# The way down of a SwiGLU FFN in seven products over all tiles of h, with GpSimd forming the sums

## The chip, the cores and the metric

The kernel runs on one core of a Trainium2 chip. The metric is the device time of one execution in microseconds. TensorE (PE in the profile) multiplies matrices into PSUM; VectorE (DVE), ScalarE (ACT) and GpSimd (POOL) do elementwise work; SyncE (SP) holds the queue from which every transfer of this kernel is issued, in order.

## The reference

One layer of a hybrid encoder: two token mixers, a gated merge, a layer norm, and the FFN to which the change belongs.

```python
x = layer_norm(DEEPNORM_ALPHA * x + mix, ln1_g[l], ln1_b[l])
gu = x @ w_ffn_in[l]
g, u = jnp.split(gu, 2, axis=-1)
ffn = (jax.nn.silu(g) * u) @ w_ffn_out[l]
x = layer_norm(DEEPNORM_ALPHA * x + ffn, ln2_g[l], ln2_b[l])
```

x is 1024 x 1024, h = silu(g) * u is 1024 x 2816, all in float32. A product of float32 precision is made of three products of rounded parts: each operand a is split into a high part (a cast on ScalarE to the format fp32r) and a low part (a subtraction on VectorE), and hi*hi, hi*lo and lo*hi are added up in PSUM.

## The kernel before, in words

Sequence, model width and FFN width are cut into tiles of 128. A slot is an SBUF buffer of 128 x 1024 float32; slots come in tags (`bw`, `pt`, `yt`, `kp`, `op`, `xt`, `gt` and the group `QKV` of four tags with two each), and a tile gets one when an earlier tile of its tag is done with. A bank is a PSUM buffer of 128 x 512 (tags `mm`, `sc`, `tr`, `pv`; eight in all). A scheduler at build time fixes the order of each engine's queue: it takes the program's order as priority and moves up what its own estimate shows to be ready. On the chip each queue then runs in that order and waits by semaphores.

**The way up** (`up_steps`, `pair_steps`, `run_pairs`) makes h transposed, tile f = 0..21: rows are 128 features of h, columns the 1024 positions. Tile f of the gate and tile f of the up half form a pair of 2 x 2 blocks, multiplied by the seven products of Strassen's scheme in Winograd's form, in the order 1, 2, 6, 5, 7, 3, 4; each is 12 TensorE products of 128 x 128 by 128 x 512. Names in the profile: `sxf`, `syf` and `szf` are the banks (`sxf` takes products 1, 6, 7, 4, `szf` 5 and 3, `syf` 2), `wLf` and `wRf` the loaded weights, `wlf`, `waf`, `wbf` and `wcf` their split operands, `gt` and `h` the results. Between products ScalarE or VectorE read the bank, which goes on adding up. `right` and `left` load and prepare the weights of the next two pairs. A finished h tile is stored to `h_dr`.

**The way down** multiplies h by `w_ffn_out` (2816 x 1024). The 22 tiles of h are taken in six groups (2, then five times 4). For a group, its h tiles (`wr_h`) and the matching rows of `w_ffn_out` (`wr_fo`) are loaded and split whole (`wh_`, `wl_`); then for each of the 8 row tiles and both column halves one bank (`fps`) takes all products of the group, and VectorE adds it to `acc_t`, which held x1, the FFN's input (slots `op`, loaded from `x1_dr`). After the last group each row tile is normalised by `layer_norm` and stored: statistics, a power on GpSimd, a scaling on ScalarE, the addition of `ln2_b` on GpSimd; the last tile takes a quick form on VectorE.

Of the kernel before, what the change touches and what calls it, by code (L numbers as in the profile page):

```python
# [11 lines left out]
F32 = mybir.dt.float32  # L12
# [12 lines left out]
N_REL = 513  # L25
D_FF = 2816
NF = D_FF // P
ALPHA = 2.0 ** 0.25
EPS = 1e-5
BIG = 1e30  # L30
# [16 lines left out]
def hybrid_trunk_kernel(ctx: ExitStack, tc, x, xt, w_in, b_gate, rel_bias, w_proj,  # L47
# [14 lines left out]
    def slot(tag, name, dtype=F32):  # L62
        return pool.tile([P, 1024], dtype, tag=tag, name=name, bufs=SLOTS[tag])
# [32 lines left out]
    g_dr = dram("g_dr", 16)  # L96
    m_dr = dram("m_dr", 8)
    x1_dr = dram("x1_dr", 8)
    h_dr = dram("h_dr", NF)
    rel_dr = dr.tile([8, 896], F32, name="rel_dr")  # L100

    def split(dst_h, dst_l, src):
        nc.scalar.copy(dst_h, src)  # L103
        nc.vector.tensor_tensor(dst_l, src, dst_h.bitcast(F32), ALU.subtract)  # L104
# [283 lines left out]
    def load_w(srcs, name, raw, hl, lo_eng):  # L388
        r = raw(f"wr_{name}")
        hi = hl(f"wh_{name}", F32R)  # L390
        lo = hl(f"wl_{name}", F32R)
        srcs = srcs if isinstance(srcs, list) else [(slice(0, 1024), srcs)]
        for cs, src in srcs:
            dma(r[:, cs], src)
        nc.scalar.copy(hi, r)  # L395
        lo_eng.tensor_tensor(lo, r, hi.bitcast(F32), ALU.subtract)
        return hi, lo

    def of(tag):
        return lambda name, dtype=F32: slot(tag, name, dtype)  # L400
# [404 lines left out]
    def right_f(f):  # L805
        prep_right(Wf[f], f"f{f}", w_ffn_in[NF + f], ("bw", "pt")[f % 2],
                   "op" if f == 1 else None)
        if f:
            prep_last(Wf[f], f"f{f}", "op")

    def up_steps(f):
# [12 lines left out]

        def done(name, acc):
            if name == "11":
                nc.scalar.activation(c("11"), c("11"), AF.Silu)
            elif name == "12":
                nc.vector.tensor_tensor(c("12"), c("12"), c("11"), ALU.mult)
            elif name == "21":  # L830
                h = tl["h"]
                nc.scalar.activation(h[:, HI], acc, AF.Silu)
                nc.vector.tensor_tensor(h[:, HI], h[:, HI], c("22"), ALU.mult)
                dma(h_dr[f], h)

        return pair_steps(f"f{f}", Wf[f], ops_1, c, done, "pv" if f == 2 else "mm")

# [31 lines left out]
    down_tags = [("bw",) * 2 + ("kp",) * 2, QKV + ("bw", "bw", "pt", "pt"), ("xt",)]  # L869
    for gi, (f0, f1) in enumerate(groups):  # L870
        hs = []
        tags = down_tags[0 if gi == 0 else 1 + gi % 2]
        take = lambda name, dtype: cycle(tags, name, dtype)
        for f in range(f0, f1):
            hs.append(load_w(h_dr[f], f"h{f}", of("gt"), take, nc.vector) +
                      load_w(w_ffn_out[f * P:(f + 1) * P, :], f"fo{f}", of("gt"), take,
                             nc.vector))
        if f1 == NF:
            norm2 = [bcast(src, slot("yt", f"ln2{n}")) for src, n in ((ln2_g, "g"), (ln2_b, "b"))]
        for tt in range(8):  # L880
            if gi == 0:
                dma(acc_t[tt], x1_dr[tt])
            ts_ = slice(tt * P, (tt + 1) * P)
            for hf, cs in enumerate((LO, HI)):
                acc = bank("mm" if hf == 0 else "tr", f"fps{gi}_{tt}_{hf}")
                mm3(acc, [(hh[:, ts_], hl[:, ts_], oh[:, cs], ol[:, cs])
                          for hh, hl, oh, ol in hs])
                if gi == 0:
                    nc.vector.scalar_tensor_tensor(acc_t[tt][:, cs], acc_t[tt][:, cs], ALPHA,
                                                   acc, ALU.mult, ALU.add)  # L890
                else:
                    nc.vector.tensor_tensor(acc_t[tt][:, cs], acc, acc_t[tt][:, cs], ALU.add)  # L892
            if f1 == NF:
                layer_norm(acc_t[tt], *norm2, f"2_{tt}", tt == 7,
                           lambda cs: dma(out[tt * P:(tt + 1) * P, cs], acc_t[tt][:, cs]))


def granules(w):
# [31 lines left out]
```

## Time and profile before

| | |
|---|---|
| median of 3 runs (lowest, highest) | 1504.65 us (1503.48, 1505.57) |
| span of the profiled execution | 1506.8 us |
| TensorE / VectorE / ScalarE / GpSimd busy | 97% / 63% / 43% / 17% |
| mean granted TensorE clock | 0.994 |
| way up, last products before the way down | to 1259.3 us |
| way down, first to last product | 1259.3 to 1498.4 us |
| bytes moved | 202 MB, 134 GB/s over the span |

The execution that was profiled has no time of its own beside its span; the runs' times are of other executions. In a row of the profile's groups stand the line of the kernel, the engine, the operation, output and inputs by name, the count, and durations; `[idle <- X]` is how long the engine stood still before it and what ended that. A row of the stages gives the stretch, its length, then busy time and count for PE, PEld (weight loads), DVE, ACT and POOL, the granted clock, and the share and rate of the transfers.

### The profile page before, as it was taken

The numbers are of one execution on the slowest core, as the hardware profiler recorded it, in microseconds if no ns is written. First come the engines' busy times: TensorE is split into PE (matmuls) and PEld (weight loads), VectorE is DVE, ScalarE is ACT, GpSimd is POOL, SyncE is SP. The second block draws the span as 40 slices with busy tenths as digits, with TensorE's granted clock in tenths as the row PEclk, the third lists the DMA queues.
The fourth block names the chain that finished last, engine by engine and source line by source line (L and its number), as shares of the span: only waits on it lengthen the run. The fifth ranks groups of instructions, "written<-read, shape, count | busy, mean of one in ns | idle before, by whom it ended". The sixth has DMA issues, their size and how long they took to land.

```text
span 1506.8 us, 18782 instructions
## 1 busy us (share of the span) xinstructions
PE 1463.4 (97%) x6860; PEld 1204.9 (80%) x6860; DVE 945.1 (63%) x1533; ACT 645.2 (43%) x1112; POOL 255.8 (17%) x296
## 2 busy tenths in 40 slices
PE   8999999999999999999999899999999999999997
PEld 6788888787777888787887688888888888888886
DVE  8865556376677677786849975555555547354437
ACT  6444444476676567765303543333333334021201
POOL 0000000243345556840014000000000000000016
PEclk9999999999999999999999999999999999999999
DMA  6555554755554545657502132222222248032202
GB/s 210 168 169 168 167 168 159 237 162 142 154 154 126 156 135 172 209 183 277 197 6 93 57 140 85 84 84 84 84 84 81 80 151 303 29 126 98 71 5 107
DMA packets 59325, 202.09 MB, mean 134 GB/s; under 512 B 7632, under 2 KB 7632, under 8 KB 59232
## 3 DMA queue, kind: packets, MB, share of 16 engines
q1 hardware_dynamic: 59232, 200.89, 41.0%
q8 instruction: 54, 0.88, 0.2%
q14 instruction: 39, 0.32, 0.1%
HBM read 141.06 MB, written 59.80 MB: 133 GB/s over the span
## 4 chain that ended last, share of the span: by engine, by line
PE 82%; DVE 8%; ACT 3%; DMA 3%; issue 2%; POOL 1%; SPq 0%; POOLq 0%; DVEq 0%; ACTq 0%
PE sxf L165 15%; PE sxp L165 9%; PE szf L165 8%; PE gps L412 5%; PE fps L113 5%; PE fps L111 5%; PE fps L110 5%; PE szp L165 5%; PE syf L165 4%; PE syp L165 2%; PE yAps L600 2%; PE tp_b L550 2%; PE ops L113 2%; PE ops L111 2%; PE ops L110 2%
## 5 line engine op out<-in xcount | busy, mean ns | idle before, releaser
L744 POOL TENSOR_TENSOR mv<-mv,neghalf 128x1 f32<-128x1 f32 x16 | 23.7, 1479 | 763.4 <-DVE mv L743 763.4
L110 PE MATMUL fps<-wh_fo,wh_h 128*128 128x512 f32 x352 | 136.9, 389 | 0.0
L111 PE MATMUL fps<-wl_fo,wh_h 128*128 128x512 f32 x352 | 136.9, 389 | 0.0
L113 PE MATMUL fps<-wh_fo,wl_h 128*128 128x512 f32 x352 | 136.9, 389 | 0.0
L892 DVE TENSOR_TENSOR x<-fps,x 128x512 f32<-128x512 f32 x80 | 55.1, 689 | 97.0 <-PE fps L113 97.0
L529 POOL TENSOR_TENSOR w_b<-w_b,kp_b 128x511 f32<-128x511 f32 (+3 forms) x96 | 99.3, 1038 | 64.9 <-DVE kp_b L527 39.1
L527 DVE TENSOR_TENSOR_SCAN kp_b<-kp_b,ident_ps 128x384 f32<-128x384 f32 (+6 forms) x88 | 78.4, 891 | 4.6
L412 PE MATMUL gps<-xh,wl_g 128*128 128x512 f32 x192 | 80.9, 421 | 0.0
L412 PE MATMUL gps<-xh,wh_g 128*128 128x512 f32 x192 | 80.5, 419 | 0.0
L412 PE MATMUL gps<-xl,wh_g 128*128 128x512 f32 x192 | 80.5, 419 | 0.0
L111 PEld LDWEIGHTS fps<-wl_fo,wh_h 128*128 128x128 f32 x352 | 66.1, 188 | 13.8
L110 PEld LDWEIGHTS fps<-wh_fo,wh_h 128*128 128x128 f32 x352 | 66.1, 188 | 13.7
L113 PEld LDWEIGHTS fps<-wh_fo,wl_h 128*128 128x128 f32 x352 | 66.1, 188 | 13.7
L395 ACT CAST wh_h<-wr_h 128x1024 fp32r<-128x1024 f32 x22 | 23.1, 1052 | 118.7 <-PE fps L111 93.6
L519 ACT ACTIVATE kp_b<-sc_b 128x512 f32<-128x512 f32 (+3 forms) x96 | 48.3, 503 | 45.2 <-PE sc_b L456 33.8
L104 DVE TENSOR_TENSOR pt_b<-tp_b,pt_b 128x512 fp32r<-128x512 f32 (+1 forms) x96 | 51.0, 542 | 19.2 <-ACT pt_b L103 19.0
L494 POOL TENSOR_SCALAR w_a<-w_a,st_a 128x640 f32<-128x640 f32 (+2 forms) x64 | 46.4, 728 | 82.7 <-DVE st_a L493 69.9
L165 PE MATMUL szf<-x1S63h,wcf 128*128 128x512 f32 x176 | 57.8, 389 | 0.0
L103 ACT CAST pt_b<-tp_b 128x512 fp32r<-128x512 f32 (+1 forms) x96 | 47.8, 498 | 21.6 <-PE tp_b L550 21.4
L550 PE MATMUL tp_b<-ident,w_b 128*128 128x128 f32 x288 | 48.8, 277 | 4.2 <-DVE pt_b L104 1.8
L104 DVE TENSOR_TENSOR pt_a<-tp_a,pt_a 128x512 fp32r<-128x512 f32 (+1 forms) x96 | 45.6, 485 | 10.3 <-ACT pt_a L103 10.2
L178 DVE TENSOR_TENSOR gt<-sxf,gt 128x512 f32<-128x512 f32 x22 | 15.1, 688 | 58.5 <-PE sxf L165 58.5
(1535 smaller groups left out, 4192.8 us busy)
## 6 DMA issues: line engine op xcount, KB each, us to landing
wLf<-in_w_ffn_in_dram SPq DMA_DIRECT2D x22, 512.0 KB, 3.6
wRf<-in_w_ffn_in_dram SPq DMA_DIRECT2D x22, 512.0 KB, 3.6
h_dr<-h SPq DMA_DIRECT2D x22, 512.0 KB, 2.6
wr_h<-h_dr SPq DMA_DIRECT2D x22, 512.0 KB, 4.3
wr_fo<-in_w_ffn_out_dram SPq DMA_DIRECT2D x22, 512.0 KB, 4.3
v_dr<-v SPq DMA_DIRECT2D x16, 512.0 KB, 3.5
kl<-k_dr SPq DMA_DIRECT2D x32, 256.0 KB, 6.2
v<-v_dr SPq DMA_DIRECT2D x16, 512.0 KB, 3.2
```

The lines of the kernel that those rows point to most:

```text
L103: nc.scalar.copy(dst_h, src)
L104: nc.vector.tensor_tensor(dst_l, src, dst_h.bitcast(F32), ALU.subtract)
L110: mm(acc, lh, rh, start=(i == 0), stop=False)
L111: mm(acc, lh, rl, start=False, stop=False)
L113: mm(acc, ll, rh, start=False, stop=(i == n))
L165: mm(acc, lw[:, ks], rx, start=(first and kt == i == 0), stop=(kt == 3 and i == 2), skip_group_check=not first)
L412: mm(acc, lw[:, ks], rx[k][:, cs], start=(k == j == 0), stop=(k == KT - 1 and j == 2))
L519: nc.scalar.activation(kp[:, c0:e], sc[:, 0:n], AF.Sigmoid, scale=-1.0)
L527: nc.vector.tensor_tensor_scan(kp[:, s0:e], kp[:, s0:e], ident_ps()[:, 0:e - s0], kp[:, s0 - 1:s0], ALU.mult, ALU.bypass)
L529: nc.gpsimd.tensor_tensor(be[:, m0:e], be[:, m0:e], kp[:, m0 - 1:e - 1], ALU.mult)
L550: tr(tp[:, (qb - lo_q) * P:(qb - lo_q + 1) * P], wt[qb - q0][:, (kb - qb) * P:(kb - qb + 1) * P], ident)
L892: nc.vector.tensor_tensor(acc_t[tt][:, cs], acc, acc_t[tt][:, cs], ALU.add)
```

## The change

h is no longer multiplied group by group. Its 22 tiles and the 22 row blocks of `w_ffn_out` form 11 pairs, i = 0..10; the two tiles of a pair, each cut into two halves of the positions, are the 2 x 2 blocks on the left, the two row blocks, each cut into two halves of the columns, those on the right. The seven products are made one after another, each over all 11 pairs: a step is one pair in one product, 4 row tiles x 3 = 12 TensorE products. Product 1 is kept in four banks (`xbank`), in which products 6, 7 and 4 go on adding; product 2 and then product 5 take the other four (`zbank`), and 3 goes on from 5. After each product the four banks are added into `acc_t`. In product 4 the row tiles come one after another, each over all 11 pairs.

The left sums are made on GpSimd at the end of each second pair of the way up (`left_sums`), and seven halves of 128 x 512 a pair are stored to `left_dr`, in place of whole tiles to `h_dr`. The right sums are made on GpSimd from the loaded row blocks, in their own place (`right_sums`). Each step loads its left half (two to a `gt` slot) and splits both operands into slots `kp`, `QKV` and others (`split_left`, `split_right`). h of the even tiles from 4 on lies in a `bw` slot.

The core of the diff:

```diff
+NP2 = NF // 2
+ORDER = (1, 2, 6, 5, 7, 3, 4)
...
+    def left_sums(i):
+        ha, hb = h_of.pop(2 * i), h_of.pop(2 * i + 1)
+        sa, sb = slot("op", f"sa{i}"), slot("op", f"sb{i}")
+        add = nc.gpsimd.tensor_tensor
+        add(sb[:, LO], ha[:, LO], ha[:, HI], ALU.subtract)
+        add(sa[:, LO], ha[:, HI], hb[:, HI], ALU.add)
+        add(sa[:, HI], sa[:, LO], ha[:, LO], ALU.subtract)
+        add(sb[:, HI], hb[:, LO], sa[:, HI], ALU.subtract)
+        for p, t in ((1, ha[:, LO]), (2, hb[:, LO]), (4, hb[:, HI]), (5, sa[:, LO]),
+                     (6, sa[:, HI]), (7, sb[:, LO]), (3, sb[:, HI])):
+            dma(left_dr[p, i], t)
...
-                    tl["h"] = slot("yt", f"h{f}")
+                    tl["h"] = slot("bw" if f % 2 == 0 and f > 2 else "yt", f"h{f}")
...
-                dma(h_dr[f], h)
+                if f % 2:
+                    left_sums(f // 2)
...
-    groups = [(0, 2), (2, 6), (6, 10), (10, 14), (14, 18), (18, 22)]
...
+    row_tags = iter([("xt",)] * 16 + [("bw",)] * 6)
+    steps = [(p, i) for p in ORDER for i in range(NP2)]
...
+    def right_sums(s):
+        p, i = steps[s]
+        tt = nc.gpsimd.tensor_tensor
+        a, b = rows[0][i], rows[1][i]
+        if p == 2:
+            tt(a[:, LO], a[:, HI], a[:, LO], ALU.subtract)
+        elif p == 6:
+            t = t2[i] = slot("kp", f"t2_{i}")[:, LO]
+            tt(t, b[:, HI], a[:, LO], ALU.subtract)
+            tt(b[:, LO], b[:, LO], t, ALU.subtract)
+        elif p == 5:
+            tt(a[:, HI], b[:, HI], a[:, HI], ALU.subtract)
...
+    def split_left(s):
+        p, i = steps[s]
+        tags = next(wide) if p == 4 else next(first_tags, QKV)
+        ops["l", s] = split_to(tags, f"dl{p}_{i}", raw_l.pop((p, i)))
...
+    def triple(acc, s, mt, first, last):
+        l, r = ops["l", s], ops["r", s]
+        lh, ll = (l[:, o + mt * P:o + (mt + 1) * P] for o in (0, HW))
+        for n, (lw, rx) in enumerate(((lh, r[:, LO]), (lh, r[:, HI]), (ll, r[:, LO]))):
+            mm(acc, lw, rx, start=(first and n == 0), stop=(last and n == 2),
+               skip_group_check=steps[s][0] not in (1, 2, 5))
...
+    AHEAD = dict(load=9, sums=4, split=3)
+    base = {p: n * NP2 for n, p in enumerate(ORDER)}
...
+    def feed(s):
+        p, i = steps[s]
+        advance("load", s + AHEAD["load"] + (NP2 if p in (5, 7, 3) else 0), load)
+        advance("sums", s + AHEAD["sums"], right_sums)
+        for d in range(AHEAD["split"] + 1):
+            advance("l", s + d, split_left)
+            advance("r", s + d, split_right)
...
+    for s, (p, i) in enumerate(steps[:base[4]]):
+        feed(s)
+        if p == 3:
+            advance("l", base[4] + i, split_left)
+            advance("r", base[4] + i, split_right)
...
+        banks = zbank if p in (2, 5, 3) else xbank
+        for mt in range(4):
+            triple(banks[mt], s, mt, p in (1, 2, 5) and i == 0, i == NP2 - 1)
...
+    for mt in range(4):
+        for i in range(NP2):
+            triple(xbank[mt], base[4] + i, mt, False, i == NP2 - 1)
+        take(4 + mt, LO, xbank[mt], True)
+        end_row(4 + mt)
```

Three places where the order of the queues is another. The first is the way up around pair 12. SyncE's queue before, one store to each pair (the number behind `wLf`, `wRf` and `h` is f):

```order
L124 DMA wLf15_9794<-in_w_ffn_in_dram 128x1024
L137 DMA wRf15_9885<-in_w_ffn_in_dram 128x1024
L834 DMA h_dr11_160<-h11_9562 128x1024
L124 DMA wLf16_9919<-in_w_ffn_in_dram 128x1024
L137 DMA wRf16_10010<-in_w_ffn_in_dram 128x1024
L834 DMA h_dr12_161<-h12_9687 128x1024
```

SyncE's queue now (in `left_dr` the first number is the product, the second the pair of tiles; `sa` and `sb` are the sums):

```order
L140 DMA wRf14_9880<-in_w_ffn_in_dram 128x1024
L827 DMA left_dr1_5_184<-h10_9547 128x512
L827 DMA left_dr7_5_188<-sb5_9729 128x512
L827 DMA left_dr2_5_185<-h11_9671 128x512
L827 DMA left_dr4_5_190<-h11_9671 128x512
L827 DMA left_dr5_5_187<-sa5_9728 128x512
L827 DMA left_dr6_5_186<-sa5_9728 128x512
L827 DMA left_dr3_5_189<-sb5_9729 128x512
L127 DMA wLf15_9914<-in_w_ffn_in_dram 128x1024
L140 DMA wRf15_10017<-in_w_ffn_in_dram 128x1024
```

The load of `wLf15` stood ahead of the store of h11 and now stands behind the seven stores of tiles 10 and 11. ScalarE's queue in pair 12, before:

```order
L182 COPY gt12_9633<-sxf12_9620 128x512
L103 CAST wcf14_9776<-wRf14_9760 128x512
L103 CAST wlf15h_9796<-wLf15_9794 128x1024
L827 ACTIVATE gt12_9633<-gt12_9633 128x512
L191 COPY h12_9687<-sxf12_9620 128x512
L195 COPY gt12_9633<-szf12_9689 128x512
```

ScalarE's queue in pair 12 now:

```order
L185 COPY gt12_9754<-sxf12_9741 128x512
L106 CAST wlf14h_9792<-wLf14_9790 128x1024
L846 ACTIVATE gt12_9754<-gt12_9754 128x512
L106 CAST wcf14_9896<-wRf14_9880 128x512
L194 COPY h12_9808<-sxf12_9741 128x512
L106 CAST wlf15h_9916<-wLf15_9914 128x1024
L198 COPY gt12_9754<-szf12_9810 128x512
```

The cast of `wlf15h` moved from behind product 1 to the last place ahead of the copy out of the bank `szf`, and `wcf14`, whose slot a tile `sa` or `sb` had, stands right ahead of the copy of h12.

The second place is the opening of the way down in SyncE's queue. Before, the loads of x1 stood between those of the first groups:

```order
L882 DMA x1_2_10841<-x1_dr2_143 128x1024
L882 DMA x1_3_10842<-x1_dr3_144 128x1024
L394 DMA wr_fo2_11013<-in_w_ffn_out_dram 128x1024
L882 DMA x1_4_10843<-x1_dr4_145 128x1024
L394 DMA wr_h3_11019<-h_dr3_152 128x1024
```

Now (`rows0` and `rows1` are the row blocks of a pair, `raw1_9`, here in the tile of `raw1_8`, the left half of product 1 and pair 9):

```order
L827 DMA left_dr6_10_221<-sa10_11002 128x512
L827 DMA left_dr3_10_224<-sb10_11003 128x512
L977 DMA x1_0_11015<-x1_dr0_141 128x1024
L977 DMA x1_1_11016<-x1_dr1_142 128x1024
...
L977 DMA x1_7_11022<-x1_dr7_148 128x1024
L905 DMA raw1_8_11061<-left_dr1_9_212 128x512
L896 DMA rows0_10_11106<-in_w_ffn_out_dram 128x1024
L905 DMA raw1_10_11108<-left_dr1_10_219 128x512
L896 DMA rows1_0_11128<-in_w_ffn_out_dram 128x1024
L905 DMA raw2_0_11130<-left_dr2_0_150 128x512
```

All eight loads of x1 now stand together, behind the last stores of the sums and ahead of the operands of product 1's pairs 9 and 10 and of product 2. The third place is TensorE in product 3. Before, the products of a bank stood in one row to the end:

```order
L110 MATMUL fps5_7_1_12434<-wh_fo20_12126,wh_h20_12120 128x512
L111 MATMUL fps5_7_1_12434<-wl_fo20_12127,wh_h20_12120 128x512
L113 MATMUL fps5_7_1_12434<-wh_fo20_12126,wl_h20_12121 128x512
L110 MATMUL fps5_7_1_12434<-wh_fo21_12138,wh_h21_12132 128x512
L111 MATMUL fps5_7_1_12434<-wl_fo21_12139,wh_h21_12132 128x512
```

Now (`dn5` are the banks of products 5 and 3, `dn1` those of 1, 6, 7 and 4; `dr3_4` and `dl3_4` are the right and left operand of product 3, pair 4):

```order
L945 MATMUL dn5_3_11848<-dr3_3_12294,dl3_3_12291 128x512 x3
L945 MATMUL dn1_0_11090<-dr4_0_12342,dl4_0_12318 128x512 x3
L945 MATMUL dn1_0_11090<-dr4_1_12362,dl4_1_12359 128x512 x2
L945 MATMUL dn1_1_11091<-dr4_0_12342,dl4_0_12318 128x512
L945 MATMUL dn1_0_11090<-dr4_1_12362,dl4_1_12359 128x512
L945 MATMUL dn5_0_11845<-dr3_4_12321,dl3_4_12297 128x512
L945 MATMUL dn5_1_11846<-dr3_4_12321,dl3_4_12297 128x512
```

Ahead of pairs 4, 5, 6 and 7 of product 3 stand 7, 4, 5 and 4 products of product 4; the rest of the way down keeps the order of the program.

More of the change, by code (lines that the diff above doesn't have):

```diff
@@ L98, in hybrid_trunk_kernel @@
     x1_dr = dram("x1_dr", 8)
-    h_dr = dram("h_dr", NF)
+    left_dr = {(p, i): dr.tile([P, HW], F32, name=f"left_dr{p}_{i}")
+               for i in range(NP2) for p in ORDER}
     rel_dr = dr.tile([8, 896], F32, name="rel_dr")
@@ L864, in hybrid_trunk_kernel @@
               first=3)
-    groups = [(0, 2), (2, 6), (6, 10), (10, 14), (14, 18), (18, 22)]
     acc_t = [slot("op", f"x1_{tt}") for tt in range(8)]
[L869 to L895, printed above, removed]
@@ new lines, in triple, with take @@
+    def triple(acc, s, mt, first, last):
[4 more added lines that the diff above has]
+               skip_group_check=steps[s][0] not in (1, 2, 5))
+    def take(tt, half, bank_, first):
+        dst = acc_t[tt][:, half]
+        if first:
+            nc.vector.scalar_tensor_tensor(dst, dst, ALPHA, bank_, ALU.mult, ALU.add)
+        else:
+            nc.vector.tensor_tensor(dst, bank_, dst, ALU.add)
```

56 lines of the change are left out of this document (added).

## The prediction

> **What bounds the kernel now.** I read the page first, then busy time by stage, then the rows of the tile fps, then the waits. The page's busy row and chain row:
>
> ```profile
> span 1506.8 us, 18782 instructions
> PE 1463.4 (97%) x6860; PEld 1204.9 (80%) x6860; DVE 945.1 (63%) x1533; ACT 645.2 (43%) x1112; POOL 255.8 (17%) x296
> PE 82%; DVE 8%; ACT 3%; DMA 3%; issue 2%; POOL 1%; SPq 0%; POOLq 0%; DVEq 0%; ACTq 0%
> ```
>
> TensorE is busy for 97% of the span and makes 82% of the chain. Whether this holds where the change is, the stages tell (way up, then three pieces of the way down):
>
> ```profile
> core 0: us, PE busy (x) PEld busy (x) DVE busy (x) ACT busy (x) POOL busy (x), PEclk, DMA share, GB/s
> 1060.00:1160.00 100.00, 100.00 (x443) 82.81 (x442) 51.56 (x67) 33.77 (x47) 0.00 (x0) 1.00 0.25 82
> 1259.00:1283.00 24.00, 24.00 (x108) 19.87 (x107) 21.85 (x28) 10.08 (x10) 0.00 (x0) 1.00 0.83 286
> 1326.00:1370.00 44.00, 44.00 (x196) 36.44 (x195) 21.71 (x27) 9.27 (x9) 0.00 (x0) 1.00 0.34 111
> 1456.00:1500.00 44.00, 42.83 (x189) 35.12 (x188) 32.19 (x54) 8.06 (x7) 26.39 (x14) 1.00 0.18 72
> ```
>
> Both stages are TensorE from end to end at full clock; VectorE is half free on the way up, GpSimd wholly. So the time of the way down is its number of products times their pitch:
>
> ```profile
> L110 PE MATMUL fps<-wh_fo,wh_h x352: 389/389/389, 1259.3 to 1498.0; 128*128 128x512 f32 x176
> L113 PE MATMUL fps<-wh_fo,wl_h x352: 388/389/389, 1259.8 to 1498.4; 128*128 128x512 f32 x176
> 1232.27 2.72 PE sxf L165 x12
> 1498.61 0.24 PE fps L113
> 1498.87 0.70 DVE x L892
> ```
>
> The 389 ns overlap. Twelve products of the same shape took 2.72 us, a pitch of 0.2267; 3 x 352 = 1056 products x 0.2267 = 239.4, and from 1259.3 to 1498.85 lie 239.5. There is no gap to win, only products to leave out.
>
> **The change part by part.**
>
> *Products removed.* Now 7 products x 11 pairs x 4 row tiles x 3 = 924 of the same 128x512 form, 132 fewer: 132 x 0.2267 = 29.9 us, all on the path. The tail behind the last product (1506.8 - 1498.85 = 8.0) keeps its steps: one addition, statistics, power, two scalings, the store. Cost 0.
>
> *Splits and additions.* 154 half-width splits replace 44 full ones, and 28 bank takes replace 96:
>
> ```profile
> L396 DVE TENSOR_TENSOR wl_h<-wr_h,wh_h x22: 1216/1225/1228, 1234.8 to 1423.1; 128x1024 fp32r<-128x1024 f32 x22
> L104 DVE TENSOR_TENSOR wcf<-wRf,wcf x22: 681/684/693, 852.6 to 1208.5; 128x512 fp32r<-128x512 f32 x22
> L103 ACT CAST wcf<-wRf x22: 608/622/631, 835.9 to 1207.6; 128x512 fp32r<-128x512 f32 x22
> L892 DVE TENSOR_TENSOR x<-fps,x x80: 681/692/692, 1284.0 to 1498.9; 128x512 f32<-128x512 f32 x80
> ```
>
> VectorE: before 44 x 1.225 + 96 x 0.69 = 120 us, now (154 + 28) x 0.69 = 126 of a stage of 209.5. A step of twelve products lasts 2.72 and needs 1.37 on VectorE and 1.24 on ScalarE. Eight buffers hold the operands of four steps, so a split may start three steps (8.2 us) ahead; cast and subtraction take 1.3. Cover 6.9 us: cost 0.
>
> *Products 3 and 4.* There the left operands of all of product 3 are taken before its right ones, so the right ones of pairs 4, 5, 6 and 7 get a buffer only when the step before ends: four holes of 0.62 + 0.68 = 1.3, 5.2 us in all. The order fills them with 7, 4, 5 and 4 products of product 4, 20 x 0.2267 = 4.5. These are moved, not added. If each filler's operands are there, 0.7 stays; if none is, 5.2. I take 0.7, nearer to the lower end, since a filler's load has over a step (2.72) from its free buffer to its use against 2.6 for twice its bytes (the store row below).
>
> *Left sums on GpSimd.* 44 on the way up. The nearest row is its multiplication of two 128x512 tensors; how it meets VectorE is seen where both have two inputs in SBUF:
>
> ```profile
> 448.12 1.28 POOL L529 TENSOR_TENSOR w_b<-w_b,kp_b 128x512 f32<-128x512 f32 x1 [0.38 <-ACT kp_b L519]
> 818.35 1.28 DVE L745 SCALAR_TENSOR_TENSOR acc<-acc,mv,ln1g 128x1024 f32<-128x1024 f32 x1
> 821.29 2.40 POOL L753 TENSOR_TENSOR acc<-acc,ln1b 128x1024 f32<-128x1024 f32 x1 [1.26 <-ACT acc L752]
> 821.44 3.33 DVE L745 SCALAR_TENSOR_TENSOR acc<-acc,mv,ln1g 128x1024 f32<-128x1024 f32 x1
> 813.23 1.22 DVE L104 TENSOR_TENSOR wlf2l<-wLf,wlf2h 128x1024 fp32r<-128x1024 f32 x1
> 813.78 2.93 POOL L753 TENSOR_TENSOR acc<-acc,ln1b 128x1024 f32<-128x1024 f32 x1 [1.27 <-ACT acc L752]
> ```
>
> L745 took 3.33 in place of 1.28: it began behind L753 and ended 1.1 after that one's end (821.29 + 2.40 = 823.69). At 813.78 GpSimd was the one that waited, 2.93 for 2.40. So the two shut each other out: a sum costs 1.28 plus the rest of a VectorE instruction, and keeps VectorE for 1.28 at most.
>
> The sums are off the path themselves; their stores are not, quite. SyncE's queue is in order. After each second pair it holds seven stores, the last of them waiting for the last sum, and behind them the next loads. Where the next even pair begins, its time 0, three rows matter in ScalarE's queue: wlf15h (cast of such a load), then the copy of gt12 out of the bank that product 3 goes on to fill. In the trace of before, pair 12:
>
> ```profile
> 1068.91 0.62 PE L165 MATMUL sxf<-x1A,wlf12h 128*128 128x512 f32 x2
> 1071.11 0.68 DVE L833 TENSOR_TENSOR h<-h,gt 128x512 f32<-128x512 f32 x1
> 1074.85 1.05 ACT L103 CAST wlf15h<-wLf 128x1024 fp32r<-128x1024 f32 x1
> 1079.99 0.59 ACT L195 COPY gt<-szf 128x512 f32<-128x512 f32 x1 [2.08 <-PE szf L165]
> 1082.51 0.39 PE L165 MATMUL szf<-x1S63h,wcf 128*128 128x512 f32 x1
> wLf<-in_w_ffn_in_dram SPq DMA_DIRECT2D x22, 512.0 KB, 3.6
> h_dr<-h SPq DMA_DIRECT2D x22, 512.0 KB, 2.6
> ```
>
> Time 0 is 1068.9. h11 is whole at 2.9 (1071.79). Three chained sums: the first waits for VectorE's split of wcf13 to about 3.5, then 3 x 1.28 gives 7.4; issue of the last store and of the load to 7.9; landing 3.6 later, 11.5; cast 1.05, 12.6; copy 0.59, 13.2. Product 3 needs it at 13.6 (1082.51). Slack 0.4 us, where before the cast was done at 7.0. Bounds: nothing, if the load lands in 3.6; about 1.0 an even pair if the sums wait for VectorE twice more (2 x 0.7). It is met in pairs 4, 6, ... 18, eight times. I take 0.13 each, 1.0 in all, near the lower end because VectorE has little to do between 3.5 and 6.5. The copy of h12, which waits through wcf14 for the stores of sa, comes to 7.4 - 1.28 + 0.4 + 2.6 + 0.62 + 0.59 = 10.3 against 10.9: covered.
>
> The rule of the Trainium skill that speaks against this placing stands in its GPSIMD Engine Reference, section "Engine selection": plain two-input arithmetic belongs on VectorE, GpSimd being about twice as slow. The rows above give 1.28 against 0.68 and agree. By the rule the sums would fit on VectorE, half free here, and the chain would be 1.8 us shorter; the total would then lack the 1.0 above. The sum here goes by GpSimd.
>
> *Right sums on GpSimd.* 44 x 1.28 = 56 us, from the first split right operand on. By the order the sums for product 6 run four pairs ahead of their splits, and these three steps ahead of TensorE: cover 4 x 2.72 = 10.9 against 2 x 1.28 + 1.37 - 2.72 = 1.2 us too much a step over seven steps, 8.4. Cost 0.
>
> *Loads at the opening.* Stores and reloads of halves move 20.2 MB each way, 11.5 before. What queues at the opening: behind the last sums (about 5.5 us after the first product) eight tiles of x1, 4.2 MB, then 1.8 MB more up to the left half of step 11. The rate when a queue stands:
>
> ```profile
> 1245.00:1250.00 5.00, 5.00 (x23) 4.13 (x22) 1.83 (x2) 2.48 (x3) 0.00 (x0) 1.00 0.98 365
> 1250.00:1255.00 5.00, 5.00 (x23) 4.13 (x22) 1.92 (x2) 1.69 (x4) 0.00 (x0) 1.00 0.98 383
> 1270.00:1275.00 5.00, 5.00 (x24) 4.14 (x23) 5.00 (x7) 2.10 (x2) 0.00 (x0) 1.00 0.73 247
> ```
>
> 6.0 MB at 365 take 16.5: there at 5.5 + 16.5 + 2 = 24 with the landing, needed at 11 x 2.72 - 1.3 = 28.6. Cover 4.6; at 247 it would be 4 late. I take 0, since in the first two windows too several loads stood in the queue.
>
> *Sum.* -29.9 + 0.7 + 1.0 = -28.2. The profiled execution spans 1506.8, 2.15 above the median of the runs (1504.65; 1503.48 to 1505.57), so I carry the difference over: 1504.65 - 28.2 = **1476.5 us**.
>
> **The rivals.**
>
> A. *Loads late behind the stores of the sums* on the way up. For it: slack 0.4, against 3.6 us of landing that was measured with one load on its way. Against: no other transfer of size stands there. With 1.0 in each of eight pairs: 1504.65 - 28.2 + 7 = 1483.5.
>
> B. *The opening is bound by the transfers.* At 247 GB/s the left half of step 11 is 4 late, and the next four steps, 0.79 MB each, take 3.2 for 2.72, 2 more: 1482.5. For it the 247, against it 365 and 383.
>
> C. *GpSimd and VectorE shut each other out on the way down* and their sum binds. In products 1, 2 and 6: 56 for sums, 66 splits x 0.69 = 46, 12 takes x 0.69 = 8, together 110 against 33 x 2.72 = 90: 20 more, 1496.7. For it the 3.33 and 2.93 above; against it the lead of the sums. The Trainium skill's page SBUF — State Buffer, section "Who interferes with whom", states the mechanism: whichever starts first holds the shared port for its whole instruction. The rows agree; it would decide only where no lead is left.
>
> D. *Slower than before:* the same place as A, with a gap long enough to lower the clock:
>
> ```profile
> 852.00:856.00 4.00, 2.19 (x5) 1.80 (x6) 3.62 (x6) 3.26 (x4) 0.00 (x0) 0.50 0.37 118
> 853.81 0.79 PE L165 MATMUL sxf<-x1S63h,wbf0h 128*128 128x512 f32 x1 [3.28 <-ACT x1S63h L103]
> 854.40 1.05 PE L165 MATMUL syf<-x1A,wlf2h 128*128 128x512 f32 x2
> ```
>
> A gap of 3.28 here stood before a clock of 0.50 and some eleven products at twice their pitch, 2.5 us. From gaps of 3.3 on each even pair would lose 5.8, eight times 46: 1504.65 - 29.2 + 46, about 1522. It decides if a sum takes 2.5, twice its row: nothing in the trace does that.
>
> **How the numbers follow.** Forecast 0.66, its own range 1474 to 1479 (1474.7 with no stall at all). A 0.17, B 0.08, C 0.05, D 0.04. Forecast and A hold 0.83, so the range ends where A and B end: 1474 to 1486. Within 0.2%, 3 us, which is about what this measurement can tell from no change, ends only a case between C and D: 0.02. Slower 0.04, faster 0.94.
>
> **What would show it.** In the profile after: 924 products on dn, first to last 209.5 to 212 us apart, TensorE full in each window; eight idle times before szf products on the way up, released by ScalarE's copy of gt, at most 0.3 each (over 0.8: A); no wait of a dn product for a load in steps 9 to 16 (else B); a VectorE subtraction of 1.3 to 2 where a sum runs, without a wait of TensorE behind it (else C); four waits below 0.6 in product 3. I am wrong if TensorE idles by more than 10 us between 880 us and its last product.

## The result and the profile after

The changed kernel takes 1489.33 us (median of 4 runs, 1487.28 to 1489.71) against 1505.11 for the kernel before (4 runs, 1503.48 to 1508.28): ratio 0.9888, 95% interval 0.9872 to 0.9904. It is 15.8 us faster where 28.2 were forecast, and lies above the range that ended at 1486. The profiled execution spans 1485.5. The page's busy row and chain row:

```profile
span 1485.5 us, 19020 instructions
PE 1434.5 (97%) x6728; PEld 1176.0 (79%) x6728; DVE 997.1 (67%) x1575; ACT 689.2 (46%) x1222; POOL 391.3 (26%) x384
PE 72%; DVE 11%; DMA 5%; POOL 4%; issue 4%; ACT 3%; SPq 1%; DVEq 0%; POOLq 0%; ACTq 0%
```

TensorE's busy time fell by 28.9 us, close to the 29.9 that the products left out are worth. But its share of the chain fell from 82% to 72%, VectorE's rose from 8% to 11% and GpSimd's from 1% to 4%: something else now sets the end in places. Busy time by stretch shows where (columns as in the prediction):

```profile
1240.00:1280.00 40.00, 40.00 (x178) 33.13 (x177) 22.70 (x24) 13.22 (x24) 23.31 (x16) 1.00 0.84 316
1280.00:1320.00 40.00, 37.17 (x155) 28.28 (x154) 38.28 (x35) 17.51 (x30) 32.36 (x20) 1.00 0.71 255
1320.00:1360.00 40.00, 40.00 (x178) 33.11 (x178) 34.63 (x42) 17.02 (x30) 17.81 (x12) 1.00 0.31 96
1440.00:1480.00 40.00, 31.59 (x140) 25.83 (x138) 31.57 (x44) 8.07 (x7) 27.65 (x14) 0.92 0.20 79
```

And the products among the rows of the tile `dn` (minimum, median and maximum in ns, then first and last start):

```profile
L945 PE MATMUL dn<-dr,dl x924: 387/389/506, 1255.8 to 1471.2; 128*128 128x512 f32 x185
```

From 1280 to 1320 TensorE got through 155 products where a full stretch holds 178, and there VectorE is busy nearly all the time (38.28 of 40) and GpSimd for 32.36. The last product starts at 1471.2 and the span ends at 1485.5. So I divided each profiled execution into three lengths: the way up (first product on `syf` to the first on `dn`, before `fps`), the way down (start of the first to start of the last product), and the tail (from there to the end of the span). The last column tells where left sums / right sums are made; the runs are those of the next section.

| kernel | way up | way down | tail | median us | sums |
|---|---|---|---|---|---|
| before | 429.3 | 239.1 | 8.4 | 1505.1 to 1505.6 | none |
| after | 430.3 | 215.4 | 14.3 | 1489.33 | GpSimd / GpSimd |
| e1 | 431.4 | 210.2 | 14.3 | 1486.16 | GpSimd / VectorE |
| e2 products 3, 7 swapped | 430.9 | 233.4 | 8.5 | 1501.75 | GpSimd / GpSimd |
| e3 product 6's sums unused | 432.3 | 221.0 | 14.3 | 1499.98 (one run) | GpSimd / GpSimd |
| e4 rows 0 to 3 quick | 430.8 | 216.0 | 13.3 | 1488.74 | GpSimd / GpSimd |
| e5 x1 loaded later | 431.6 | 212.5 | 14.7 | 1488.04 (one run) | GpSimd / GpSimd |
| e6 | 428.7 | 213.2 | 14.3 | 1483.13 (one run) | VectorE / GpSimd |
| e7 swapped, norms spread | 431.0 | 221.4 | 8.6 | 1492.12 | GpSimd / VectorE |
| e8 as e7, x1 later | 428.9 | 222.7 | 9.0 | 1489.05 | VectorE / VectorE |
| e9 | 429.1 | 210.1 | 14.4 | 1481.45 | VectorE / VectorE |
| e10 as e9, x1 later | 428.8 | 210.7 | 14.6 | 1481.69 | VectorE / VectorE |
| e11 as e9, rows 2, 6 quick | 428.8 | 210.1 | 14.7 | 1483.16 | VectorE / VectorE |
| e12 swapped, norms late | 429.0 | 220.6 | 8.6 | 1487.66 | VectorE / VectorE |

923 pitches of 0.2267 are 209.2 us, so after the change the way down has 6.2 us of holes. What lies ahead of the way up (the token mixers) is not changed, and its length differs by up to 5.7 us between executions (`syf` starts from 824.9 to 830.6); the three lengths leave that out. Each of them is that of one profiled execution. From before to after they change by +1.0 (+1.9 with the mean of the seven executions that make the left sums on GpSimd, 431.2), -23.7 and +5.9: together -15.9 with the mean, against -15.8 in the medians.

**First loss: 6.2 us of holes on the way down.** GpSimd's, VectorE's and TensorE's instructions in product 2 (start, duration):

```profile
1287.15 1.74 POOL L916 TENSOR_TENSOR rows<-rows,t 128x512 f32<-128x512 f32 x1
1287.66 0.68 DVE L951 SCALAR_TENSOR_TENSOR x<-x,dn 128x512 f32<-128x512 f32 x1
1288.26 1.18 DVE L107 TENSOR_TENSOR dl<-raw,dl 128x512 fp32r<-128x512 f32 x1
...
1295.66 1.74 POOL L918 TENSOR_TENSOR rows<-rows,rows 128x512 f32<-128x512 f32 x1
1296.17 1.78 DVE L107 TENSOR_TENSOR dr<-rows,dr 128x512 fp32r<-128x512 f32 x1
1296.31 3.02 PE L945 MATMUL dn<-dr,dl 128*128 128x512 f32 x12 [0.38 <-DVE dl L107]
1297.37 1.74 POOL L916 TENSOR_TENSOR rows<-rows,t 128x512 f32<-128x512 f32 x1
1297.87 1.78 DVE L107 TENSOR_TENSOR dl<-raw,dl 128x512 fp32r<-128x512 f32 x1
1299.70 3.02 PE L945 MATMUL dn<-dr,dl 128*128 128x512 f32 x12 [0.38 <-DVE dl L107]
```

Each sum and each split is recorded at 1.74 to 1.78 in place of 1.28 and 0.68, and both start anew every 1.70 us: one waits out the other, by turns. A step needs two splits, so it lasts 3.39 (1296.31 to 1299.70) and not 2.72. The addition of a bank at 1287.66 kept its 0.68 beside a running sum: one of its inputs lies in PSUM.

**Second loss: 5.9 us of tail.** GpSimd in the kernel before (L744 is the power, L753 the addition of `ln2_b`):

```profile
1479.11 1.46 POOL L744 TENSOR_TENSOR mv<-mv,neghalf 128x1 f32<-128x1 f32 x1 [0.32 <-DVE mv L743]
1481.83 2.40 POOL L753 TENSOR_TENSOR x<-x,ln2b 128x1024 f32<-128x1024 f32 x1 [1.26 <-ACT x L752]
1484.62 1.45 POOL L744 TENSOR_TENSOR mv<-mv,neghalf 128x1 f32<-128x1 f32 x1 [0.39 <-DVE mv L743]
```

GpSimd, VectorE and ScalarE in the changed kernel (now L747 and L756; L748 and L755 are the scalings):

```profile
1448.17 1.52 POOL L747 TENSOR_TENSOR mv<-mv,neghalf 128x1 f32<-128x1 f32 x1 [107.41 <-DVE mv L746]
...
1467.82 2.39 POOL L756 TENSOR_TENSOR x<-x,ln2b 128x1024 f32<-128x1024 f32 x1 [1.26 <-ACT x L755]
1468.28 3.01 DVE L748 SCALAR_TENSOR_TENSOR x<-x,mv,ln2g 128x1024 f32<-128x1024 f32 x1
1470.17 1.53 POOL L747 TENSOR_TENSOR mv<-mv,neghalf 128x1 f32<-128x1 f32 x1
1471.73 1.15 ACT L755 ACTIVATE x<-x,mv 128x1024 f32<-128x1024 f32 x1 [3.99 <-POOL mv L747]
1472.96 2.34 POOL L756 TENSOR_TENSOR x<-x,ln2b 128x1024 f32<-128x1024 f32 x1 [1.26 <-ACT x L755]
1473.46 2.92 DVE L748 SCALAR_TENSOR_TENSOR x<-x,mv,ln2g 128x1024 f32<-128x1024 f32 x1
1475.26 1.53 POOL L747 TENSOR_TENSOR mv<-mv,neghalf 128x1 f32<-128x1 f32 x1
...
1480.34 0.55 POOL L747 TENSOR_TENSOR mv<-mv,neghalf 128x1 f32<-128x1 f32 x1
```

Before, a row of the result was complete every 5.44 us (24 products), and its norm kept GpSimd for 5.1, with 0.3 to spare ("0.32 <-DVE"). Now four rows are complete together, when product 3 ends (about 1446), and four more follow at 7.5 us (33 products) up to 1471.6: eight norms while product 4 has 25 us left, since 20 of its 132 products went ahead as fillers. The eight powers start from 1448.17 to 1480.34, 4.6 us apart on average. GpSimd no longer waits for VectorE's statistics; for the last rows it goes round at 5.1 us each: addition 2.34, then VectorE's scaling of a later row, which had waited for that addition (about 1.1), then the power, which had waited for that scaling (0.4), then ScalarE's scaling (1.26 of idle). The last row's power is due at about 1474 (its input is written at 1473.39) and starts at 1480.34.

**Third loss: 1 to 3 us on the way up.** VectorE's waits for the loads of `wRf` from the third pair on (us in total, times, longest): the kernel before, the changed one, and e6, in this order.

```profile
DVE taf L140 <- DMA wRf<-in_w_ffn_in_dram: 11.0, 17, 1.7
```

```profile
DVE taf L143 <- DMA wRf<-in_w_ffn_in_dram: 46.4, 18, 3.9
```

```profile
DVE taf L143 <- DMA wRf<-in_w_ffn_in_dram: 18.2, 16, 1.8
```

One place in e5, whose way up is that of the changed kernel, where TensorE waits (SyncE, VectorE and TensorE in order of time):

```profile
1075.80 0.33 SPq L140 DMA_DIRECT2D wRf<-in_w_ffn_in_dram  x1
...
1081.34 0.69 DVE L143 TENSOR_TENSOR taf<-wRf,wLf 128x512 f32<-128x512 f32 x1 [4.49 <-DMA wRf<-in_w_ffn_in_dram]
1083.88 0.68 DVE L181 TENSOR_TENSOR gt<-sxf,gt 128x512 f32<-128x512 f32 x1
1084.62 0.73 PE L168 MATMUL sxf<-x1A,wbf12h 128*128 128x512 f32 x2 [0.66 <-DVE gt L181]
```

The loads stand behind the seven stores of the sums in SyncE's queue (here the last store was issued at 1074.72); VectorE's four sums of the loaded weights wait for them, and behind these stands the addition of the bank `sxf`, which product 4 needs.

### The profile page after: what moved, and what is told of

Read it like the earlier page. It is cut to its first block, busy times and chain, and to the rows that moved or that the text cites. A ratio compares the mean times of both kernels' runs of the same rounds, so it can differ in the third digit from the quotient of the medians.

```text
span 1485.5 us, 19020 instructions
## 1 busy us (share of the span) xinstructions
PE 1434.5 (97%) x6728; PEld 1176.0 (79%) x6728; DVE 997.1 (67%) x1575; ACT 689.2 (46%) x1222; POOL 391.3 (26%) x384
## 4 chain that ended last, share of the span: by engine, by line
PE 72%; DVE 11%; DMA 5%; POOL 4%; issue 4%; ACT 3%; SPq 1%; DVEq 0%; POOLq 0%; ACTq 0%
PE sxf L168 14%; PE dn L945 10%; PE sxp L168 9%; PE szf L168 7%; PE gps L415 6%; PE szp L168 5%; PE syf L168 3%; PE syp L168 2%; PE ops L116 2%; PE ops L114 2%; PE tp_b L553 2%; PE ops L113 2%; PE yAps L603 2%; DVE kp_b L530 1%; PE tp_a L553 1%
## 5 line engine op out<-in xcount | busy, mean ns | idle before, releaser
L945 PE MATMUL dn<-dr,dl 128*128 128x512 f32 x924 | 213.0, 391 | 2.8 <-DVE dl L107 1.8
L945 PEld LDWEIGHTS dn<-dr,dl 128*128 128x128 f32 x924 | 172.3, 188 | 43.4 <-DVE dl L107 4.6
L107 DVE TENSOR_TENSOR dl<-raw,dl 128x512 fp32r<-128x512 f32 x77 | 68.7, 904 | 33.6 <-ACT dl L106 33.3
L106 ACT CAST dl<-raw 128x512 fp32r<-128x512 f32 x77 | 47.3, 623 | 83.4 <-PE dn L945 67.2
L747 POOL TENSOR_TENSOR mv<-mv,neghalf 128x1 f32<-128x1 f32 x16 | 23.3, 1454 | 237.2 <-DVE mv L746 233.2
L821 POOL TENSOR_TENSOR sb<-h 128x512 f32<-128x512 f32 x11 | 18.9, 1720 | 205.1 <-PE syf L168 131.6
L497 POOL TENSOR_SCALAR w_a<-w_a,st_a 128x640 f32<-128x640 f32 (+2 forms) x64 | 46.4, 728 | 81.8 <-DVE st_a L496 69.0
L107 DVE TENSOR_TENSOR dr<-rows,dr 128x512 fp32r<-128x512 f32 x66 | 55.4, 847 | 16.1 <-ACT dr L106 16.0
L822 POOL TENSOR_TENSOR sa<-h,h 128x512 f32<-128x512 f32 x11 | 17.5, 1589 | 145.0 <-PE sxf L168 105.5
L106 ACT CAST pt_a<-tp_a 128x512 fp32r<-128x512 f32 (+1 forms) x96 | 40.4, 424 | 27.2 <-PE tp_a L553 26.5
L494 ACT ACTIVATE w_a<-w_a,st_a 128x640 f32<-128x640 f32 (+2 forms) x64 | 44.6, 699 | 17.2 <-DVE st_a L489 16.4
```

The lines of the kernel that those rows point to most:

```text
L494: nc.scalar.activation(s[:, 0:w], s[:, 0:w], AF.Exp, bias=st[:, m:m + 1], scale=-1.0, accum_out=st[:, 2:3])
L497: nc.gpsimd.tensor_scalar(s[:, 0:w], s[:, 0:w], st[:, 3:4], 0.0, ALU.mult, ALU.add)
L945: mm(acc, lw, rx, start=(first and n == 0), stop=(last and n == 2), skip_group_check=steps[s][0] not in (1, 2, 5))
```

## The experiments

**e1: the right sums on VectorE.** One word is changed; the order of every other instruction stays.

```diff
     def right_sums(s):
         p, i = steps[s]
-        tt = nc.gpsimd.tensor_tensor
+        tt = nc.vector.tensor_tensor
```

> The 44 right sums of the way down are made by VectorE in place of GpSimd; nothing else moves. Theory 1 (the two engines shut each other out: in products 2 and 6 a split and a sum take turns every 1.70 us, so two splits a step need 3.4 against 2.72): the sums take 0.68 each on VectorE and the splits go back to 0.68; first to last product 210 to 211 us in place of 215.4, time about 1484.5. Theory 2 (the loads of the opening are late behind the eight tiles of x1): the gaps stay, 214 to 216 us, about 1489. Theory 3 (VectorE alone has too much to do there): 215 or more, 1489 or more. The tail behind the last product stays at 14 us in all three.

Ratio to before 0.9871 (0.9842 to 0.9899), 1486.16 us. The stretch, and the tile:

```profile
1280.00:1320.00 40.00, 40.00 (x179) 33.10 (x178) 35.71 (x58) 18.45 (x32) 0.00 (x0) 1.00 0.76 276
```

```profile
L945 PE MATMUL dn<-dr,dl x924: 387/389/501, 1259.7 to 1469.9; 128*128 128x512 f32 x185
```

179 products in place of 155, and 210.2 us in place of 215.4: theory 1. VectorE does 58 instructions in 35.71 us where it did 35 in 38.28. The transfers keep their engines as busy (0.76 against 0.71), so that alone does not hold up TensorE. The runs' times do not tell e1 from the changed kernel (the two intervals overlap); the reading rests on the trace, and on e9, e10 and e11, whose right sums are on VectorE too and whose way down is 210.1 to 210.7.

**e2: products 3 and 7 swapped.** Rows 0 to 3 are then complete 30 us earlier.

```diff
-ORDER = (1, 2, 6, 5, 7, 3, 4)
+ORDER = (1, 2, 6, 5, 3, 7, 4)
...
-        if p == 3:
+        if p == 7:
             advance("l", base[4] + i, split_left)
...
-            if p == 7:
+            if p == 5:
                 norm2 = [bcast(src, slot("yt", f"ln2{n}"))
```

> Product 3 is made before product 7 (order 1, 2, 6, 5, 3, 7, 4), so the four rows that it completes are normalised 30 us earlier. Theory 1 (the tail of 14 us is a backlog: four rows are complete at once when only product 4 is left, and GpSimd's queue takes power, addition, power, addition at 5.1 us a row): the tail falls to 8 us as before the change, time about 1483. Theory 2 (a row's norm is itself longer here because the two engines shut each other out): the tail stays at 12 to 14, about 1488. If the norms' additions hold up the splits of product 7, first to last product grows from 215.4 by up to 3.

The tail is 8.5 us, as theory 1 has it. But the way down grew by 18 us, not by up to 3, and the time is 1501.75, ratio 0.9974 (0.9958 to 0.9990). TensorE in product 7:

```profile
1429.05 3.78 PE L945 MATMUL dn<-dr,dl 128*128 128x512 f32 x8 [6.24 <-DVE dr L107]
1433.53 1.19 PE L945 MATMUL dn<-dr,dl 128*128 128x512 f32 x4 [0.71 <-ACT dr L106]
1437.62 3.78 PE L945 MATMUL dn<-dr,dl 128*128 128x512 f32 x8 [2.90 <-DVE dr L107]
```

The 8 products at 1429.05 take 3.78, twice their pitch: the granted clock had fallen (0.50 over 1429 to 1433, 0.87 over 1400 to 1440). What the 18 us consist of, e7 and e12 show in part.

**e3: product 6's sums made, but not used.** The sums go to a buffer that nobody reads, and product 6's right operands are split from the row blocks as loaded (so products 6 and 4 multiply other numbers).

```diff
-            t = t2[i] = slot("kp", f"t2_{i}")[:, LO]
-            tt(t, b[:, HI], a[:, LO], ALU.subtract)
-            tt(b[:, LO], b[:, LO], t, ALU.subtract)
+            t = slot("kp", f"t2_{i}")
+            t2[i] = b[:, HI]
+            tt(t[:, LO], b[:, HI], a[:, LO], ALU.subtract)
+            tt(t[:, HI], b[:, LO], t[:, LO], ALU.subtract)
```

> GpSimd still makes the 22 sums of product 6, into a buffer that nobody reads; the right operands of products 6 and 4 are split from the row blocks as loaded, so no split waits for these sums. Theory 1 (the engines shut each other out): VectorE's subtractions still take 1.7 beside them, first to last product stays at 214 to 217 us. Theory 2 (TensorE waits because the sums themselves come late): 210 to 211.

```profile
1306.42 1.77 DVE L107 TENSOR_TENSOR dr<-rows,dr 128x512 fp32r<-128x512 f32 x1
...
1330.20 1.78 DVE L107 TENSOR_TENSOR dl<-raw,dl 128x512 fp32r<-128x512 f32 x1
```

The holes do not go, so theory 2 falls. The size was missed: 221.0, above the 214 to 217. With no split to wait for, GpSimd made its sums without a pause to 1341 (after: to 1311), and VectorE stayed at 1.77 a split for nearly as long. More sums beside splits, more loss.

**e4: the quick norm for rows 0 to 3.**

```diff
-        layer_norm(acc_t[tt], *norm2, f"2_{tt}", tt == 7,
+        layer_norm(acc_t[tt], *norm2, f"2_{tt}", tt < 4 or tt == 7,
```

> Rows 0 to 3 get the quick form of the last norm (scaling and addition in one pass on VectorE, GpSimd makes only the power). Theory 1 (the tail is the backlog in GpSimd's queue): GpSimd keeps three additions; VectorE then has 4 x 4.3 us from 1446.7 on and the other rows 3.5 each, so the tail falls to 10 to 12 us, time 1485.5 to 1487.5. Theory 2 (VectorE is the one that is late): its work grows by 4 x 1.4 = 5.7, the tail is 16 or more, time 1491 or more. First to last product stays at 215.4.

Ratio 0.9886 (0.9868 to 0.9904): not told apart from after. The tail went from 14.3 to 13.3, between what the two theories gave. The stretch of the norms:

```profile
1440.00:1480.00 40.00, 33.43 (x148) 27.36 (x146) 30.84 (x52) 3.45 (x3) 17.44 (x10) 0.98 0.21 79
```

GpSimd was relieved of 10 us (17.44 against 27.65), but VectorE stayed as busy (30.84 against 31.57), and from 1446 on it never paused until row 7 came. So the expectation's theory 1, in the form "GpSimd's queue alone", is too narrow: both engines are full, and here the work moved from one to the other gained 1.0 us of tail and nothing in the time.

**e5: x1 loaded one tile to a step.** In the trace of after, ScalarE stood still for 6.4 us before a cast in product 1, waiting for a left half whose load stood behind the eight tiles of x1, and GpSimd behind VectorE's splits:

```profile
1279.31 0.62 ACT L106 CAST dl<-raw 128x512 fp32r<-128x512 f32 x1 [6.39 <-DMA raw<-left_dr]
1282.09 1.68 POOL L912 TENSOR_TENSOR rows<-rows 128x512 f32<-128x512 f32 x1 [5.36 <-DVE dr L107]
```

```diff
-    for tt in range(8):
-        dma(acc_t[tt], x1_dr[tt])
     for s, (p, i) in enumerate(steps[:base[4]]):
         feed(s)
+        if s < 8:
+            dma(acc_t[s], x1_dr[s])
```

> The eight loads of x1 are issued one to a step in steps 0 to 7 of product 1, in place of all together ahead of them; the sums stay on GpSimd. Theory 1 (the loads only took GpSimd's lead: between 1275 and 1282 us it waited for row blocks that stood behind x1, and then made 16 sums without a pause, beside which VectorE gets one split in 1.70 us): with the lead kept the sums are spread out and first to last product is 211 to 213 us in place of 215.4. Theory 2 (GpSimd and VectorE together have too much for products 1, 2 and 6, whatever the loads do): 215 to 216.

212.5 us: theory 1. (What the load held up was a split's left half, and GpSimd only through the splits, not by a row block as the expectation says.) The loads took the lead that the splits had, and while sums run beside the splits VectorE does not make it up again. With the lead kept, 3.3 us of holes are left; with the sums on VectorE 0.9 to 1.5, whether x1 comes early or late (e9, e10). The loads of x1 also started later than the prediction has it, 9.8 us after the first product and not 5.5. GpSimd made right sums first, and the store of the last left sum stands ahead of x1 (trace of after):

```profile
1259.59 1.62 POOL L918 TENSOR_TENSOR rows<-rows,rows 128x512 f32<-128x512 f32 x1
1261.17 1.29 POOL L822 TENSOR_TENSOR sa<-h,h 128x512 f32<-128x512 f32 x1
...
1263.91 1.29 POOL L824 TENSOR_TENSOR sb<-h,sa 128x512 f32<-128x512 f32 x1
...
1265.61 4.38 SPq L977 DMA_DIRECT2D x<-x_dr  x8
```

So e1's edit had a second effect: with no right sums on GpSimd, the left half of step 9 came sooner, cast 21.3 us after the first product in place of 23.5. The next run, e6, has the same gain there (21.4) with the right sums still on GpSimd. The two casts, e1's and e6's:

```profile
1280.97 0.62 ACT L106 CAST dl<-raw 128x512 fp32r<-128x512 f32 x1 [4.17 <-DMA raw<-left_dr]
```

```profile
1275.31 0.62 ACT L106 CAST dl<-raw 128x512 fp32r<-128x512 f32 x1 [4.31 <-DMA raw<-left_dr]
```

With loads equally early the way down is 213.2 in e6 and 210.2 in e1: about 3 of the 5.2 us hang on the right sums alone, and about 2 on the sums together with the later loads (one trace each).

**e6: the left sums on VectorE.** `add = nc.vector.tensor_tensor` in `left_sums`.

> The 44 left sums of the way up are made by VectorE in place of GpSimd; the right sums stay. Theory 1 (a few pairs of the way up are 0.3 to 0.8 us longer than 19.05 because a sum on GpSimd holds up VectorE's addition for product 4): every pair takes 19.0 to 19.1 again, the way up is as long as before the change, 429.3 us from the first product on syf to the first on dn in place of 430.3 to 432.3. Theory 2 (the pairs are longer for the loads behind the stores of the sums): VectorE's sums are done about 1.8 us sooner, but the same chain stays, and the longer pairs stay in part.

Every pair takes 19.0 to 19.1 us, and the way up 428.7, so it fits the numbers of theory 1. But the rows above show the other mechanism: VectorE's addition was late for a load, not for a sum. The sums are done sooner on VectorE, the loads behind their stores come sooner, and what is left of the waits (18.2 in place of 46.4) lies within the slack. Part of that fall is only that VectorE makes the sums while it would have waited; and the scheduler put the load of `wLf` ahead of the last two stores (in one pair 1067.70 against 1068.30 and 1069.03), so the sums' speed and the new place of that load are not separated. All five later kernels with left sums on VectorE have 428.8 to 429.1. The way down fell too, to 213.2, as said above.

**e7 and e8: the norms spread in the swapped order.** The norms of rows 0 to 3 come after pairs 1, 3, 5 and 7 of product 7; e8 has the left sums on VectorE and the later x1 as well.

```diff
+        if p == 7 and i in (1, 3, 5, 7):
+            end_row({1: 0, 3: 1, 5: 2, 7: 3}[i])
...
-            if p == 3:
-                for mt in range(4):
-                    end_row(mt)
```

> Product 3 ahead of product 7, the norms of rows 0 to 3 one to every second pair of product 7 (after pairs 1, 3, 5 and 7) in place of together, and the right sums on VectorE. If the tail is the backlog of norms and the loss of the swapped order came only from the norms standing in a row ahead of the splits: first to last product 210 to 212 us, tail 8 us, time 1478 to 1481. If a single norm is already too long for the splits behind it (3.4 us of VectorE and up to 2.4 of shutting out, against a lead of 8.2): 213 to 218, time 1482 to 1488.

> As the run with swapped products, spread norms and the right sums on VectorE, and besides the left sums on VectorE and the loads of x1 one to a step. If the three losses are separate (sums beside splits 5.2, backlog of norms 5.9, way up 1 to 3): 1489.3 - 5.2 - 5.9 - 1.9 = 1476.3, between 1475 and 1479. If the sums overfill VectorE on the way up or at the opening: 1480 or more.

1492.12 (ratio 0.9921, 0.9905 to 0.9938) and 1489.05 (0.9901, 0.9885 to 0.9918). The tails are 8.6 and 9.0, the way down 221.4 and 222.7. For e7 both time and length lie above either forecast; e8's time lies in its second range, but not for the reason given there: its way up is 428.9, and all its waits of TensorE on the way down stand in product 7, as in e7. Spreading the norms and moving the sums took 12 of e2's 18 us away; against e1's 210.2 some 11 stayed.

**e9 and e10: all sums on VectorE, the order as in after.** e10 has the later x1 too.

> Left and right sums on VectorE, order of the products and loads as in the changed kernel. If the two effects add up: way up 429 us, first to last product 210.2, tail 14; time 1489.3 - 5.2 - 1.9 = 1482.2, between 1480.5 and 1483.5. If the sums together overfill VectorE at the opening of the way down: first to last product 212 or more, 1484 or more.

> As the run with all sums on VectorE, and the loads of x1 one to a step. If the late loads did harm only through GpSimd's lead, nothing is left for them to do: first to last product 210 to 210.5, time within 1 us of that run. If they hold up TensorE themselves: up to 1 us less.

```profile
L945 PE MATMUL dn<-dr,dl x924: 387/389/499, 1255.0 to 1465.1; 128*128 128x512 f32 x185
```

```profile
1410.00:1440.00 30.00, 30.00 (x130) 23.56 (x129) 16.35 (x27) 13.06 (x23) 0.00 (x0) 1.00 0.32 106
```

e9 comes out as forecast, 1481.45 us, ratio 0.9841 (0.9826 to 0.9856); e10 takes the same time, 1481.69, 0.9840 (0.9825 to 0.9855), with a way down of 210.7 for the 210 to 210.5 forecast. The two gains add up, and e9 beats both the kernel before and the changed one. The rows above are the products of e9 and its stretch of product 3. Of the way down 0.9 us of holes are left, and there they lie: 130 products where a full stretch of 30 us holds 133 or 134.

**e11: as e9, rows 2 and 6 quick as well** (`tt in (2, 6, 7)`).

> As the run with all sums on VectorE, and rows 2 and 6, beside 7, in the quick form. Theory 1 (in the last 30 us GpSimd's queue is the one that is late, 5.1 us a row that has an addition): two additions fewer, and the last power no longer stands behind row 6's addition; tail 10 to 11.5, time 1479 to 1480.5. Theory 2 (VectorE and GpSimd are equally full, eight norms in 30 us are too many however they are shared): tail 12.5 to 14, time 1481 to 1482.5.

Tail 14.7, time 1483.16 (ratio 0.9850, 0.9832 to 0.9868), both a little above what theory 2 gave, and theory 1 is out. In neither of the two ways tried, e4 and e11, does sharing the norms otherwise take more than 1 us off the tail.

**e12: swapped, the norms late.** Rows 0 and 1 after pairs 8 and 10 of product 7, rows 2 and 3 between the rows of product 4, all sums on VectorE.

> As the run with all sums on VectorE, products 3 and 7 swapped, the norms of rows 0 and 1 after pairs 8 and 10 of product 7, of rows 2 and 3 between the rows of product 4. Theory 1 (in product 7 the four norms stood beside the splits of two products, and that made its 8 to 11 us of waits): with two norms at its end the waits fall to 2 to 5, tail 8 to 10, time 1479 to 1483. Theory 2 (the waits come from the swapped order itself, without the norms): 8 to 11 us of waits stay, 1485 to 1488.

1487.66 (0.9874, 0.9856 to 0.9892), way down 220.6, tail 8.6: theory 2 by its numbers. TensorE:

```profile
1418.96 1.20 PE L945 MATMUL dn<-dr,dl 128*128 128x512 f32 x4 [1.83 <-ACT dr L106]
...
1426.57 2.11 PE L945 MATMUL dn<-dr,dl 128*128 128x512 f32 x8 [1.80 <-DVE dr L107]
1430.81 4.61 PE L945 MATMUL dn<-dr,dl 128*128 128x512 f32 x12 [2.13 <-ACT dr L106]
1436.13 19.11 PE L945 MATMUL dn<-dr,dl 128*128 128x512 f32 x83 [0.71 <-ACT dr L106]
```

TensorE stops in front of right operands and goes on in fours and eights. These are the holes that in after stand in product 3, with fillers from product 4. In the swapped order product 4 adds to the very banks that product 7 has not given up, so it can't fill. That reason is read from the code; one norm ran there still (the scheduler moved row 0's forward), and its part in the 11 us was not separated. Nor was that of late loads: from 1408 to 1446 ScalarE waited 5.4 us for left halves, in the trace of after 2.5.

## Why the prediction was wrong, step by step

- **Products removed, -29.9:** right. In e9 the 924 products take 210.1 us from first to last start, 0.9 over their pitch.
- **Products 3 and 4, +0.7:** right, 0.9 in e9. That the fillers are worth something the swapped order suggests, where there are none and 11 us of holes.
- **Right sums on GpSimd, cost 0:** wrong, 5.2 us (215.4 - 210.2, about 2 of them together with the next term), the largest mis-sized term but one. The mechanism was seen (rival C and its rows of 3.33 and 2.93), but its cost was set against the lead of the sums. The lead of a sum was not what ran out. The question was how many splits VectorE gets while GpSimd works without a pause: one every 1.70 us, 3.4 a step against 2.72. Rival C's 20 us were too many, since the two did not stand beside each other for all of products 1, 2 and 6. The Trainium skill's page SBUF — State Buffer, section "Who interferes with whom", calls the port pair that the two engines share an exclusive lock. The trace agrees in the main: a sum by itself takes 1.29 (1261.17), splits by themselves follow each other every 0.60 (1312.07 and 1312.67 in the trace of after), together 1.89, and beside each other both start every 1.70, so they overlap by some 0.2. The same section's remark that an instruction of VectorE with at most one input in SBUF and outside its two-port modes does not contend agrees too: L951 kept 0.68.
- **Loads at the opening, cost 0:** wrong as part of the same loss. The forecast let x1 start 5.5 us after the first product, where it started at 9.8, and asked when the left half of step 11 was there, 24 us after the first product against 28.6. The first half behind x1 was that of step 9: cast from 1279.31 on, 23.5 after the first product, and needed at 24.5. TensorE hardly waited for it, but the lead of 8.2 us that was to cover the splits was gone when GpSimd's sums began in earnest. With the lead kept (e5) 2.9 of the 5.2 come back.
- **The tail, cost 0:** wrong, +5.9, and no rival held it. The step that failed is "keeps its steps": I looked at the last row and not at how far apart the rows come. Before, 5.44 us for a norm of 5.1; after, eight norms while 25 us of products are left, and the last power starts 32.2 us after the first (1448.17 and 1480.34). e2, where rows 0 to 3 come 30 us earlier, has its tail back at 8.5.
- **Left sums on the way up, +1.0:** the size was about right (+1.9, +1.0 in the profiled execution), by luck, and e6 shows that it hangs on where the sums are made. The place was wrong: not ScalarE's cast of `wlf` and the copy out of `szf` (the waits of the profile name no product on `szf`), but the load after that one, `wRf`, and VectorE's additions behind it. The chain from the stores to the loads, rival A's, was right; I followed one of its two ends.
- **Rivals B and D** did not come: in e1 the same loads cost TensorE next to nothing (1.0 us of holes), and from pair 3 on no wait of TensorE on the way up reached 1 us.

The three sizes together: 5.5 on the way down (5.2 and 0.2 of fillers), 5.9 in the tail and 0.9 on the way up make 12.3 of the 12.8 us by which the median missed; the other 0.5 is the median of before, 1505.11 in these runs for the 1504.65 that the sum started from. The sign named for being wrong, TensorE idle by more than 10 us up to its last product, did not come (6.2 on the way down, about 1 on the way up): it left out what follows the last product, where the largest loss lay. And the placing of the sums on GpSimd, priced at 1.0 us in all, cost 7.9 (1489.33 against e9's 1481.45).

## What to carry to other kernels

When work goes to a second engine that shuts the first one out while it runs, as GpSimd's sums did VectorE's splits here, ask not what it adds up to over the stage but how fast the first one still is while both run, and whether its lead lasts that long. When an order of products is changed, write down when each row of the result becomes complete and set the distances against the time of its epilogue; a tail that was hidden by even spacing comes out when the rows arrive together. Where a queue delays two loads, follow both to the end.

## What the runs showed of the hardware that I had not expected

- GpSimd's sums and VectorE's splits settled into strict turns: a sum every 1.70 us from 1283.72 to 1311.00, 27 us on end, and beside each sum one split, recorded at 1.77 to 1.79, or at 1.18 behind the addition of a bank.
- The power on 128 x 1 takes part too: 0.55 us alone (1480.34), 1.53 beside VectorE's scaling of 128 x 1024, after whose end (1471.29 and 1476.38) it still took 0.4.
- VectorE's statistics and its additions with one input in PSUM were not lengthened by GpSimd (0.63 to 0.70 throughout the way down and the tail).
